# Trunk step: five kinds of tiles prefer the slots of the staying pool from the pools' exchange on

## The chip, the cores and the metric

The kernel runs on one core of a Trainium2 chip. Its engines work side by side, each through its own instructions in order: TensorE (PE, with its weight loads PEld), VectorE (DVE), ScalarE (ACT), GpSimd (POOL) and SyncE (SP), which here issues most of the DMA transfers. The metric is the device time of one execution in microseconds (us). Before the change it is 1383.22 us, the median of three runs (1382.85 to 1383.98).

## The reference

One layer of a hybrid decoder trunk for a prompt of 1024 rows and 8 sample rows (together NT = 1032 columns when x is held with the model dimension of 1024 on the partitions). Everything is float32.

```
h = rmsnorm(x, norm_pre) * (1 + scale) + shift
hA, cA, bA, zA, qkv, zB, beta, alpha, gA, gB = split(h @ w_in)
yA = ((bA * conv3(cA * hA)) * silu(zA)) @ w_out_a
q, k, v = split(silu(conv4(qkv)))            # 8 heads, q and k normalised
o, S = gated_delta_chunked(q, k, v, beta, g, s0)   # a recurrence over chunks
yB = (rmsnorm(o) * silu(zB)) @ w_out_b
merged = sigmoid(gA) * yA + sigmoid(gB) * yB
y = x + gate * rmsnorm(merged @ w_o, norm_post)
```

The recurrence is serial in each head: per chunk, the state S feeds a product, that feeds X and S again.

## The kernel before

**Stages.** After a start-up, the first long stage runs 48 *jobs*. A job multiplies h by 128 columns of w_in: 3 groups of 344 columns, each 24 matmuls into one of four pm_t banks (8 blocks of the model dimension, three products of high and low halves: xh·whi, xl·whi, xh·wlo). Its weights are loaded to wraw and split into whi and wlo (two buffers each). Eight heads take three jobs each (k, q, v) and their recurrences run as background work between the matmuls of later jobs. The other jobs are zB, and the 16 gate jobs for gB and gA (`gate_job`): their products are copied by ScalarE into a tile named gate, which is stored to memory (gBsc, gAsc) and read back much later. The last three jobs of all are gate jobs; their tiles are gate_9504, gate_9611 and gate_9724. The recurrence of the last head (its result is DA, its store yBsc<-DA) runs while the jobs before and the first of these three feed TensorE.

The second stage is `products`: the four parts of branch A for one group t of 128 columns are computed by a Strassen-like scheme of seven products, P1, P2, P6, P7, P4, P5, P3, on halves of rows and columns, 48 matmuls of 258 columns each, for eight groups. Their weights are loaded in four quarters to tiles wr, combined by VectorE and split to whi and wlo (`weight_load`, `weight_gen`). Their right sides are sums of blocks of x: `block_gen` builds tiles qa, qb and q1 from xh and xl, and splits them to thi and tlo. Result tiles are acc; they are combined and stored (yAsc). Meanwhile `park_gen` combines rows of yB from memory (pa_, pb_), splits them (phi, plo) and stores them (txs). Then `products_b` does the same seven products for w_out_b (rows read back to yraw, split to thi and tlo), and after it come the projection by w_out_a, the gates and w_o.

**Memory.** The tiles named so far take slots of `T4`, an object of class `Slots`. It has 7 slots t4 of 1056 columns in a pool that stays to the end, and 11 slots hb of the same width in the heads' pool bp, which also holds small tiles of the recurrence. At the start of the third last job, `to_products` drops the hb slots, releases bp, and puts a pool m into the same memory, with 22 slots sl of 1032 columns. A tile in m must wait until the last reader of whatever lay there in bp is done. `Slots.get` takes the free slot with the least key: the narrowest that is wide enough, and among equals an hb slot for the names in `LATE` and another for the rest.

**Order.** The program is written by strands that a clock model steps; `to_products` starts the strands weight_load, weight_gen and block_gen. A scheduler orders each engine's instructions afterwards, so where a tile lies decides also where its instructions stand.

Of the kernel before, what the change touches and what calls it, by code (L numbers as in the profile page):

```python
# [168 lines left out]
def hybrid_step(  # L169
# [442 lines left out]
    def start(gen):  # L612
        bg.append(Strand(gen, sched.cur.t if sched.cur else sched.clk["PE"]))
# [33 lines left out]
        return lambda: flags.get(key)  # L647

    LATE = ("gate", "lq")

    class Slots:

# [13 lines left out]
            return self.get(name, w)  # L666

        def get(self, name, w):
            i = min((i for i in self.free if i[2] >= w), key=lambda i: (i[2], ("hb" in i[1]) == (name in LATE)))
            self.free.remove(i)  # L670
            t = i[0].tile([P, i[2]], F32, tag=i[1], name=name)
            v = t[:, :w]
            self.held[id(v)] = (i, v)
            return v
# [71 lines left out]
    def drain_bg():  # L746
        force(lambda: not bg)
# [698 lines left out]
    def alloc(key, side):  # L1446
        pools[key] = tc.alloc_tile_pool(name=key, bufs=1, side=side)
        return pools[key]
# [3 lines left out]
    def weight_load(raw):  # L1452
        for key in list(range(SG, NK)) + ["B"]:
            w, n = (w_out_b, 2) if key == "B" else (w_in, 1)
            for odd, half in ((0, 0), (0, 1), (1, 0), (1, 1)):
                for g in range(n):
                    yield from when(lambda: len(raw) < 4 * n, lambda: T4.ready())
                    v = T4.get("wr", D)
                    for q in range(2):
                        c0 = (4 * g + 2 * q + odd) * P if n == 2 else ACOL[2 * q + odd] + key * P  # L1460
                        SY.dma_start(out=v[:, q * 512:(q + 1) * 512].rearrange("p (k c) -> p k c", c=P),
                                     in_=w[0, half * 512:(half + 1) * 512, c0:c0 + P]
                                     .rearrange("(k p) c -> p k c", p=P))
                    raw[key, odd, half, g] = v
                    yield

    def weight_gen(raw):

        sums = {}
        for n, (key, p, g) in enumerate(UNITS):  # L1470
            a11, a12, a21, a22 = ((key, o, hf, g) for o in range(2) for hf in range(2))
            src = {"P1": a11, "P2": a12, "P6": a11, "P7": a21, "P4": a22, "P5": None, "P3": a12}[p]
            yield from when(lambda: unit[0] >= n - 1, lambda: src is None or src in raw)
            hi_ = wpool.tile([P, NK, P], F32R, tag="whi", name="whi", bufs=2)
            lo_ = wpool.tile([P, NK, P], F32R, tag="wlo", name="wlo", bufs=2)
            hi, lo = (v.rearrange("p k c -> p (k c)") for v in (hi_, lo_))
            v = raw[src] if src else sums.pop(g)
            A.copy(out=hi, in_=v)
            yield
            tt(lo, v, hi.bitcast(F32), ALU.subtract)  # L1480
            made[key, p, g] = (hi_, lo_)
            yield
            if p == "P2":
                yield from when(lambda: a22 in raw and a21 in raw)
                s_ = wpool.tile([P, NK, P], F32, tag="wraw", name="wsum", bufs=2)
                s_ = sums[g] = s_.rearrange("p k c -> p (k c)")
                tt(s_, raw[a21], raw[a22], ALU.add)
                yield
                tt(raw[a21], raw[a11], raw[a21], ALU.subtract)
                tt(raw[a11], s_, raw[a11], ALU.subtract)  # L1490
                yield
                tt(raw[a12], raw[a12], raw[a11], ALU.subtract)
            elif p in ("P6", "P7", "P4", "P3"):
                T4.give(raw.pop(src))
# [239 lines left out]
    def to_products():  # L1734
        drain_bg()
        T4.free = [i for i in T4.free if i[0] is not bp]
        bp.release()
        T4.extend(alloc("m", "left"), "sl", NSL, NT)
        raw = {}
        for g in (weight_load(raw), weight_gen(raw), block_gen()):  # L1740
            start(g)
# [3 lines left out]

    isp = len(jobs)
    hook(isp - 3, to_products)
    hook(isp - 1, products_next)

# [128 lines left out]
    for j in range(9):  # L1878
        i, n, xr, mh, ml, held = pre.pop(j)
# [76 lines left out]
```

## Time and profile before

| what | us |
|---|---|
| median of three runs | 1383.22 |
| the profiled execution's own time | 1384.48 |
| its span in the profile | 1382.3 |
| last head's recurrence, in the span | about 722 to 743 |
| two last gate jobs and the rest of the third last | 753 to 775 |
| first product P1 begins | 775 |

The span is 1382.3 us, 2.2 less than the profiled execution's own time, and that execution is 1.26 above the median. The mean granted clock of TensorE is 0.994. Names in the profile have their numbers left out; all instructions go through one helper, so they bear the line L129 and are told apart by tiles. A row such as "A <- B" in a view of waits means that the instruction writing A waited for the one writing B.

### The profile page before, as it was taken

How to read it: one execution, taken by the hardware profiler on the slowest of the kernel's cores; microseconds unless marked ns; L12 is line 12 of the kernel's file. 1: busy time of each engine (PE TensorE's matmuls, PEld its weight loads, DVE VectorE, ACT ScalarE, POOL GpSimd, SP SyncE). 2: the span in 40 equal slices, each digit the busy share in tenths (PEclk: the TensorE clock that was granted, in tenths of full speed). 3: DMA queues.
4: the chain of work that ended last, by engine and by line, in shares of the span. 5: the costliest groups of instructions: out<-in, count | busy, mean ns of one | idle time of the engine just before them, and what ended most of it. 6: DMA issues, size and time to landing. Idle time of an engine off the chain costs nothing.

```text
span 1382.3 us, 26425 instructions
## 1 busy us (share of the span) xinstructions
PE 1347.6 (97%) x10257; PEld 1280.6 (93%) x10257; DVE 969.4 (70%) x2495; ACT 665.8 (48%) x1554; POOL 46.3 (3%) x98
## 2 busy tenths in 40 slices
PE   5999999999999999999998999999999999999997
PEld 2799999998999999999997999999999999899786
DVE  4667877676969476786645998777778867654553
ACT  5586685575757576564542534222333335332220
POOL 1000010000001000000000000000000200000000
PEclk9999999999999999999999999999999999999999
DMA  9533332332343233242442354422231866742221
GB/s 317 137 107 109 90 107 70 98 115 69 92 114 100 68 99 109 74 116 75 135 134 86 108 199 162 138 77 77 77 92 60 244 214 225 238 143 95 84 99 46
DMA packets 184928, 165.99 MB, mean 120 GB/s; under 512 B 33710, under 2 KB 158367, under 8 KB 184795
## 3 DMA queue, kind: packets, MB, share of 16 engines
q1 hardware_dynamic: 180216, 155.71, 36.7%
q0 software_dynamic: 4384, 8.52, 2.2%
q8 instruction: 81, 1.33, 0.4%
q14 instruction: 45, 0.36, 0.1%
q10 hardware_dynamic: 202, 0.08, 0.0%
HBM read 127.59 MB, written 36.91 MB: 119 GB/s over the span
## 4 chain that ended last, share of the span: by engine, by line
PE 79%; DVE 10%; DMA 5%; ACT 4%; issue 2%; SPq 1%; DVEq 0%; ACTq 0%
PE pm_t L129 54%; PE pa_t L129 22%; PE pb L129 3%; DVE wlo L129 2%; DVE kq L129 2%; DVE acc L129 1%; DVE Ts L129 1%; DVE Ttmp L129 1%; ACT junk L129 1%; DMA yAsc<-acc 1%; DMA xs<-in_x_prompt_dram 1%; SPq L129 1%; DMA Ts<-sT 1%; DVE vT L129 1%; DMA gcB<-gsc 1%
## 5 line engine op out<-in xcount | busy, mean ns | idle before, releaser
L129 PE MATMUL pm_t<-xh,whi 128*128 128x344 f32 (+1 forms) x1384 | 455.0, 329 | 4.8 <-ACT gate L129 4.4
L129 PE MATMUL pm_t<-xl,whi 128*128 128x344 f32 (+1 forms) x1384 | 435.7, 315 | 0.0
L129 PE MATMUL pm_t<-xh,wlo 128*128 128x344 f32 (+1 forms) x1384 | 435.6, 315 | 0.0
L129 PEld LDWEIGHTS pm_t<-xh,whi 128*128 128x128 f32 x1384 | 262.5, 190 | 8.2 <-ACT gate L129 4.6
L129 PEld LDWEIGHTS pm_t<-xl,whi 128*128 128x128 f32 x1384 | 262.6, 190 | 0.1
L129 PEld LDWEIGHTS pm_t<-xh,wlo 128*128 128x128 f32 x1384 | 261.9, 189 | 0.1
L129 ACT CAST whi<-wr 128x1024 fp32r<-128x1024 f32 x60 | 62.8, 1047 | 138.6 <-PE pm_t L129 67.3
L129 ACT CAST whi<-wraw 128x512 fp32r<-128x512 f32 x112 | 68.3, 626 | 57.3 <-PE pm_t L129 52.0
L129 DVE TENSOR_TENSOR wlo<-wraw,whi 128x512 fp32r<-128x512 f32 x112 | 75.8, 687 | 28.4 <-ACT whi L129 27.8
L129 PE MATMUL pm_t<-thi,wlo 128*128 128x258 f32 x304 | 85.8, 283 | 1.3 <-DVE wlo L129 1.3
L129 PE MATMUL pa_t<-thi,wlo 128*128 128x258 f32 x304 | 85.9, 283 | 0.6 <-DVE wlo L129 0.6
L129 PE MATMUL pa_t<-tlo,whi 128*128 128x258 f32 x304 | 86.0, 283 | 0.0
L129 PE MATMUL pm_t<-thi,whi 128*128 128x258 f32 x304 | 86.0, 283 | 0.0
L129 PE MATMUL pm_t<-tlo,whi 128*128 128x258 f32 x304 | 85.9, 283 | 0.0
L129 PE MATMUL pa_t<-thi,whi 128*128 128x258 f32 x304 | 85.9, 283 | 0.0
L129 DVE TENSOR_TENSOR wlo<-wr,whi 128x1024 fp32r<-128x1024 f32 x60 | 73.3, 1222 | 10.5 <-ACT whi L129 10.2
L129 PE MATMUL pa_t<-xh,whi 128*128 128x258 f32 x256 | 72.5, 283 | 0.0
L129 PE MATMUL pa_t<-xl,whi 128*128 128x258 f32 x256 | 72.5, 283 | 0.0
L129 PE MATMUL pa_t<-xh,wlo 128*128 128x258 f32 x256 | 72.3, 282 | 0.0
L129 DVE SCALAR_TENSOR_TENSOR kq<-raw,vecs,kq 128x528 f32<-128x528 f32 x96 | 70.4, 761 | 1.1 <-ACT kq L129 1.1
L129 ACT ACT_TABLE_LOAD x42 | 53.9, 1283 | 27.5 <-DVE kq L129 12.8
L129 PE MATMUL pm_t<-ylo,whi 128*128 128x344 f32 x192 | 61.7, 321 | 0.0
(377 smaller groups left out, 2956.2 us busy)
## 6 DMA issues: line engine op xcount, KB each, us to landing
wraw<-in_w_in_dram SPq DMA_DIRECT2D x48, 512.0 KB
wr<-in_w_in_dram SPq DMA_DIRECT2D x64, 256.0 KB
aw<-in_ada_w_dram SPq DMA_DIRECT2D x16, 512.0 KB
gBsc<-gate SPq DMA_DIRECT2D x8, 516.0 KB
gAsc<-gate SPq DMA_DIRECT2D x8, 516.0 KB
txs<-phi SPq DMA_DIRECT2D x8, 516.0 KB
txs<-plo SPq DMA_DIRECT2D x8, 516.0 KB
yAsc<-acc SPq DMA_DIRECT2D x8, 516.0 KB
```

Source lines behind the costliest of these rows:

```text
L129: r = f(*args, **kw)
```

## The change

From `to_products` on, five names (gate, wr, qa, qb, q1) take a free slot t4 ahead of any sl slot; before it, and for all other names, the order of slots is as it was. `EARLY` is empty until then.

```diff
     LATE = ("gate", "lq")
+    EARLY = []
...
         def get(self, name, w):
-            i = min((i for i in self.free if i[2] >= w), key=lambda i: (i[2], ("hb" in i[1]) == (name in LATE)))
+            i = min((i for i in self.free if i[2] >= w),
+                    key=lambda i: (not ("t4" in i[1] and name in EARLY), i[2], ("hb" in i[1]) == (name in LATE)))
             self.free.remove(i)
...
         T4.extend(alloc("m", "left"), "sl", NSL, NT)
+        EARLY.extend(("gate", "wr", "qa", "qb", "q1"))
         raw = {}
         for g in (weight_load(raw), weight_gen(raw), block_gen()):
             start(g)
```

Before, at that moment the narrower sl slots are preferred, so all of the named tiles lie in m. After, seven of the first ones lie in t4: wr_9475, qa_9478, qb_9479, q1_9480, gate_9504, qa_9556 and qb_9557, and then gate_9611 and qa_9701 in the slot that gate_9504 leaves. The tiles wr_9565, wr_9613, wr_9665, qa_9620, qb_9621, thi and tlo still lie in m.

ScalarE at the end of the last head. vn and DA are steps of its recurrence, whi_9627 the weights of the last gate job, whi_9694 those of P1. Before:

```order
L129 COPY vn_9427<-pa_t_9425 128x128
L129 COPY DA_7569<-pa_t_9421 128x128
L129 ACTIVATE junk_9435,so_9297<-pa_t_9421 128x128
L129 CAST whi_9627<-wraw_9469 128x512 x2
L129 COPY gate_9504<-pm_t_9471 128x344
L129 COPY gate_9504<-pm_t_9506 128x344
L129 COPY gate_9504<-pm_t_9546 128x344
L129 COPY gate_9611<-pm_t_9582 128x344
L129 CAST thi_9774<-qa_9478 128x516
```

The same place in the changed kernel, from the last steps of the head on:

```order
L129 COPY DA_7569<-pa_t_9421 128x128
L129 ACTIVATE junk_9435,so_9297<-pa_t_9421 128x128
L129 CAST whi_9627<-wraw_9469 128x512
L129 COPY gate_9504<-pm_t_9546 128x344
L129 CAST whi_9627<-wraw_9469 128x512
L129 COPY gate_9611<-pm_t_9582 128x344
L129 COPY gate_9611<-pm_t_9616 128x344
L129 CAST thi_9538<-qb_9479 128x516
L129 CAST thi_9538<-qb_9557 128x516
L129 CAST thi_9774<-qa_9478 128x516
L129 CAST thi_9774<-qa_9556 128x516
L129 CAST whi_9694<-wr_9475 128x1024
```

The first two copies to gate_9504 have moved up between the steps of the head (behind vn_9319 and ahead of vn_9391), the third and the first two of gate_9611 stand ahead of the first tile of the new pool, thi_9538.

VectorE in the change of head 6 to head 7, where S and X are steps of the recurrences and wlo the weights of a job, after the change:

```order
L129 TENSOR_TENSOR q1_9480<-qa_9478 128x516
L129 TENSOR_TENSOR qa_9478<-qb_9479,qa_9478 128x516
L129 TENSOR_TENSOR qb_9479<-qb_9479,q1_9480 128x516
L129 TENSOR_TENSOR wlo_9529<-wraw_9058,whi_9515 128x512
L129 TENSOR_TENSOR qb_9479<-qb_9479 128x516
L129 TENSOR_TENSOR wlo_9529<-wraw_9058,whi_9515 128x512
L129 TENSOR_TENSOR qa_9556<-xh_119,xl_120 128x1032
L129 COPY S_9306<-pa_t_9302 128x128
L129 TENSOR_TENSOR q1_9480<-qa_9556 128x516
L129 SCALAR_TENSOR_TENSOR X_9315<-pa_t_9311,nx_8192,vT_7734 128x128
```

Before, all of these sums stand behind the last write of DA, and behind the parking of a yB row:

```order
L129 SCALAR_TENSOR_TENSOR DA_7569<-pa_t_9458,vecs2_83,sz_8464 128x512
L129 TENSOR_TENSOR plo_10040<-pb__9809,phi_10039 128x1032
L129 TENSOR_TENSOR qa_9478<-xh_119,xl_120 128x1032
L129 TENSOR_TENSOR qb_9479<-xh_119,xl_120 128x1032
L129 TENSOR_TENSOR q1_9480<-qa_9478 128x516
L129 TENSOR_TENSOR qa_9556<-xh_119,xl_120 128x1032
L129 TENSOR_TENSOR qa_9478<-qb_9479,qa_9478 128x516
L129 TENSOR_TENSOR qb_9557<-xh_119,xl_120 128x1032
```

qa_9478 and qb_9479 themselves have moved further up, behind S_8929 and ahead of S_9111, two steps of head 6; the parking has moved down into the products.

SyncE's queue around the last head's store, before:

```order
L129 DMA gAsc_111<-gate_9124 128x1032
L129 DMA txs_114<-phi_10039 128x1032
L129 DMA out_4_dram<-S_9432 128x128
L129 DMA yBsc_113<-DA_7569 128x1024
L129 DMA txs_114<-plo_10040 128x1032
L129 DMA wr_9475<-in_w_in_dram 128x4x128 x2
L129 DMA wr_9565<-in_w_in_dram 128x4x128 x2
L129 DMA gAsc_111<-gate_9504 128x1032
```

And after:

```order
L129 DMA gAsc_111<-gate_9124 128x1032
L129 DMA out_4_dram<-S_9432 128x128
L129 DMA gAsc_111<-gate_9504 128x1032
L129 DMA yBsc_113<-DA_7569 128x1024
L129 DMA wr_9565<-in_w_in_dram 128x4x128 x2
L129 DMA wr_9613<-in_w_in_dram 128x4x128 x2
L129 DMA wr_9665<-in_w_in_dram 128x4x128 x2
L129 DMA gAsc_111<-gate_9611 128x1032
```

The store of gate_9504 now stands ahead of that of DA, and the load of wr_9475 has left the place for one some 17 transfers earlier.

## The prediction

> **What bounds the kernel now.** The page comes first: which engine is full, and whose work makes up the chain that ended last.
>
> ```profile
> PE 1347.6 (97%) x10257; PEld 1280.6 (93%) x10257; DVE 969.4 (70%) x2495; ACT 665.8 (48%) x1554; POOL 46.3 (3%) x98
> ...
> PE 79%; DVE 10%; DMA 5%; ACT 4%; issue 2%; SPq 1%; DVEq 0%; ACTq 0%
> ```
>
> TensorE is busy for 97% of the span, so a gain can only come from its waits and from time at a lower clock. The waits of TensorE, asked for in three stretches from 680 us on, show what there is to win (columns: total us, times, longest us).
>
> ```profile
> PE pm_t L129 <- ACT gate L129: 4.4, 1, 4.4
> PE pa_t L129 <- DVE wlo L129: 0.6, 1, 0.6
> PE pm_t L129 <- DVE wlo L129: 1.3, 1, 1.3
> ```
>
> The first lies in 680 to 800 us, the second in 800 to 1060, the third in 1060 to 1160. The first is by far the largest, and it is released by the very tile that the change moves. The chain of work that ended last says what the gate copy stood for.
>
> ```profile
> 748.48 1.42 DVE DA L129 x2
> ...
> 749.97 2.70 DMA yBsc<-DA
> ...
> 752.76 0.45 ACT gate L129
> ...
> 753.26 27.52 PE pm_t L129 x168
> 780.77 5.78 PE pa_t L129 x48
> ```
>
> The last head's output DA is written at 748.48, stored from 749.97 on, and only when that store has landed (2.70 us) ScalarE copies a bank of products into gate. The gate tile lies in memory that the heads' pool held; the store is the pool's last reader. The timeline shows what queues up there.
>
> ```profile
> 747.78 1.10 PE L129 MATMUL pa_t<-ident,DA 128*128 128x128 f32 x8 [0.20 <-DVE DA L129]
> ...
> 752.76 1.49 ACT L129 COPY gate<-pm_t 128x344 f32<-128x344 f32 x4 [7.94 <-DMA yBsc<-DA]
> ...
> 753.26 0.66 PE L129 MATMUL pm_t<-xh,whi 128*128 128x344 f32 x1 [4.38 <-ACT gate L129]
> ```
>
> Four copies run back to back: all four pm_t banks were full, and TensorE stood from 747.78 + 1.10 = 748.88 to 753.26, which is 4.38 us. Behind it the clock is low (windows: sum, PE, PEld, DVE, ACT, POOL busy, then granted clock, DMA share, GB/s; the second fence is of PE alone, with the clock after PE).
>
> ```profile
> 750.00:752.00 2.00, 0.00 (x0) 0.00 (x0) 1.16 (x1) 0.00 (x0) 0.00 (x0) 1.00 0.63 260
> 752.00:754.00 2.00, 0.74 (x2) 0.74 (x3) 1.22 (x2) 1.24 (x4) 0.00 (x0) 0.56 0.69 272
> ...
> 758.00:760.00 2.00, 2.00 (x11) 2.00 (x11) 2.00 (x4) 0.21 (x2) 0.00 (x0) 0.73 1.05 374
> ```
> ```profile
> 753.26:759.08 5.82, 5.82 (x20) 0.50 0.88 246
> ```
>
> A mean of 0.56 over 752 to 754 puts the fall at about 752.2, 3.4 us after TensorE's last matmul; a mean of 0.73 over 758 to 760 puts the rise at 758 + 1.08 = 759.1. So 5.8 us of matmuls ran at half clock.
>
> **The change, part by part.**
>
> *The gates leave the heads' memory.* gate_9504 and gate_9611 now take a slot of the pool that stays. Gate copies stand between the steps of the last head and before the first ScalarE operation that needs the released memory (a thi cast), so no bank is full when the transposes are done, and TensorE goes on into the second group of the last but one gate job. Removed: the 4.38 us of idle time, and with it the clock's fall. The 20 matmuls of the slow stretch took 5.82 us. At full clock they stand as these rows do:
>
> ```profile
> 764.01 0.32 PE L129 MATMUL pm_t<-xh,whi 128*128 128x344 f32 x1
> ...
> 765.89 0.32 PE L129 MATMUL pm_t<-xh,whi 128*128 128x344 f32 x1
> ```
>
> Those are 12 steps in 1.88 us, 0.157 us each; 20 x 0.157 = 3.1, so 2.7 us are lost. The chain's row gives it another way: its 168 matmuls are 120 of the gates (18.8 us at 0.157) and 48 of P1 (5.8, as the row below it), 24.6 against 27.52, so 2.9. I take 2.8. The first term is **−4.4 − 2.8 = −7.2 us**. A gap in TensorE that is left would cost its own length and, by the row of 752 to 754, nothing of the clock unless it passes some 3.4 us.
>
> The Trainium skill, TensorE: Matmul & The Clock Gate, section "What's actually happening", lets the clock rise after one busy window of about 3.4 us, from a window that runs freely; here the low stretch lasted 5.8 us. By the page's window the loss would be about half of 3.4, an estimate of 1.7, and the sum 1.1 smaller; the trace has the duration, so it decides.
>
> *The sums of x leave it too.* Here lies the second limit. Once the gates are free, VectorE has to have the sums, weights and their low halves for product P2 ready 7.2 us sooner. These rows are of VectorE's timeline before.
>
> ```profile
> 752.78 1.24 DVE L129 TENSOR_TENSOR qa<-xh,xl 128x1032 f32<-128x1032 f32 x1 [1.62 <-DMA yBsc<-DA]
> 753.93 1.23 DVE L129 TENSOR_TENSOR qb<-xh,xl 128x1032 f32<-128x1032 f32 x1
> 755.08 0.69 DVE L129 TENSOR_TENSOR q<-qa 128x516 f32<-128x516 f32 x1
> 755.68 1.23 DVE L129 TENSOR_TENSOR qa<-xh,xl 128x1032 f32<-128x1032 f32 x1
> ...
> 778.14 1.22 DVE L129 TENSOR_TENSOR wlo<-wr,whi 128x1024 fp32r<-128x1024 f32 x1
> ```
>
> A full-width operation takes 1.15 us from start to start, a half 0.60. VectorE began when the store had landed, and P2's low weights (778.14 + 1.22 = 779.4) were ready 1.4 us before P2 began at 780.77. After the change, three full operations and five halves stand earlier, before or inside the last head, 6.5 us in all, and one more full sum and three halves before the pool is free, in the 2.9 us that were idle or held the parking of another head's output. What is left between the release (about 752.8) and the end of P2's wlo is, in the changed order, 8 full operations and 15 halves: 9.2 + 9.0 = 18.2, so 771.0, or 771.5 with one wait for the first whi. P1 then starts at about 767.7 and P2 at 773.5. So 2 us are left, and this limit doesn't bind. Term: 0, and if each half-ready operand made VectorE wait, up to +2.
>
> *What they cost in the chain of heads 6 and 7.* The early operations go into engines that serve a serial recurrence, and each of their slots first waits for the store of the gate that held it. VectorE's and SyncE's rows:
>
> ```profile
> 692.66 0.35 DVE L129 SCALAR_TENSOR_TENSOR S<-S,egl,pa_t 128x128 f32<-128x128 f32 x1 [2.03 <-PE pa_t L129]
> ...
> 708.09 0.35 DVE L129 SCALAR_TENSOR_TENSOR S<-S,egl,pa_t 128x128 f32<-128x128 f32 x1 [2.19 <-PE pa_t L129]
> ...
> 723.62 0.29 DVE L129 COPY S<-pa_t 128x128 f32<-128x128 f32 x1 [2.27 <-PE pa_t L129]
> ```
> ```profile
> 689.42 0.34 SPq L129 DMA_DIRECT2D gAsc<-gate  x1
> ...
> 704.22 0.33 SPq L129 DMA_DIRECT2D gAsc<-gate  x1
> ```
>
> qa_9478 stands behind the S of 692.66 and waits for the store of 689.42; with the 2.70 us of the other store of this size it lands at 692.1, before S is done. qb_9479 stands ahead of the S of 708.09 and waits for the store of 704.22: 706.9 + 1.15 = 708.07, no slack but no loss. qa_9556 stands ahead of the copy at 723.62, which had 2.27 us of idle time before it: 1.15 fit. Bounds: 0 if all fit, 1.15 + 0.60 + 3 x 0.45 for three gate copies on ScalarE, 3.1 us, if nothing did. Since TensorE fills every step of these heads with gate matmuls, I take **+0.3**.
>
> *The weights' loads.* Of eight loads of first weights two are issued some 80 us earlier, six stay behind the release; SyncE gets no longer queue. In the products that follow, wr goes back to slots of the pool that stays, which only the five names prefer, instead of one that a result tile or a sum has just left. The chain before the second wait of TensorE, and before the third:
>
> ```profile
> 986.52 5.35 DMA yAsc<-acc
> ...
> 992.31 4.58 DMA wr<-in_w_in_dram
> ```
> ```profile
> 1109.78 6.39 DMA yAsc<-acc
> 1116.18 3.56 DMA yraw<-yBsc
> ```
>
> In the first, a weight load waited for a result tile's store, since it took that tile's slot. In the changed order it follows another wr in its slot and waits for that one's last reader, VectorE, alone: **−0.6**. In the second, a load of yB's rows waited for a result's store. The tiles yraw, yhi and ylo aren't named by the change and go on taking any slot; some loads come earlier, but a cast that waits for the store stands ahead of the weight cast. Bounds −1.3 (the wait goes) to +2.5 (most of a load of 3.56 goes into the path once more); I take **0**, the wait as it is.
>
> **Sum:** −7.2 + 0.3 − 0.6 = −7.5 us. Against the profiled execution (1384.48 us, of which 1382.3 are the span) that is 1377.0; this execution is 1.26 above the median, so beside the median of 1383.22 it is **1375.7**.
>
> **The rivals.**
>
> *A: part of the wait stays or comes back.* ScalarE works in order, and its thi casts wait for the release with the first product's whi and the third gate copy behind them; VectorE has its 18.2 us to do from the release on. If a landing later than 752.8, or waits between the two engines, made P2 late by 2 to 4 us beyond the 2 us of slack, the gain would be 3.5 to 5.5: 1377.7 to 1379.7. For it speaks that VectorE is full from 752.8 on; against it the 6.5 us that lie earlier.
>
> *B: slower, by stores in the recurrence.* At 2.70 us the stores cost nothing, but qb_9479 has no slack, and a store took 6.39 at 1109.78. At that price each of the waits of qa_9478, qb_9479 and the first gate copies puts up to 3.7 us into the path of the heads; three of them are 11, less 7.5: slower by 3.5, 1386.7. It decides from a landing of about 5.2 us on, where three waits eat the gain. Against it: a store of the same size took 2.70 in the stretch beside them, and what moves beside the early stores is one weight load of 512 KB; the 6.39 stand where the products' weights and sums are loaded.
>
> *C: it doesn't do what it says.* gate_9611 takes the same slot as gate_9504 and must wait for its store. Were that store issued behind the last head's, ScalarE would stand as before: 4 of the 4.38 us come back, the clock falls, and 1383 stays. Against it: SyncE's order has gate_9504's store ahead of yBsc's, and the copy that completes it stands between the two whi casts of this row, at about 744.4:
>
> ```profile
> 743.68 1.14 ACT L129 CAST whi<-wraw 128x512 fp32r<-128x512 f32 x2 [0.42 <-PE pm_t L129]
> ```
>
> With 0.45 for the copy and 2.70 for the store it lands by 747.7, and the free banks cover what is left.
>
> *D: more than forecast.* The third wait goes too and the chain costs nothing: 1374.1.
>
> **How the numbers follow.** Chances: forecast with its neighbourhood (gain 5.5 to 8.5) 0.60, D 0.08, A 0.18, C 0.08, B 0.06. A measurement of this kernel tells about 0.2%, 2.8 us, from no change. All of the forecast, D and nearly all of A lie below 1380.4; C and a little of A within; B above. That gives faster 0.85, same 0.09, slower 0.06. The range goes from 1373.4, which is D with 0.7 for the spread of runs, to 1380.5, A's far end with the same.
>
> **What would show it right or wrong.** In the changed profile, the wait of TensorE on ACT gate should be gone, the clock 1.00 in each window from 748 to 762, and P1's first product matmul at about 768. The S updates of heads 6 and 7 should follow each other as before; idle time of VectorE put down to gAsc would be B. TensorE waiting for DVE wlo or tlo at P2 or P6 (773 to 780) would be A. The wait near 1000 should be gone, that near 1122 there. The forecast is wrong if the gate tiles still wait for the release, or if the time comes back in a wait of TensorE later on.

## The result and the profile after

The changed kernel takes 1376.38 us, the median of six runs (1375.95 to 1376.98), beside 1383.55 for six runs of the kernel before (1382.85 to 1383.99): 7.2 us less, a ratio of 0.9948 with a 95% interval of 0.9935 to 0.9961. Its profiled execution took 1376.39 us, with a span of 1374.4. It lies on its median; that of before lies 0.9 above the median of six. The page's rows of engines and of the chain that ended last:

```profile
PE 1344.2 (98%) x10257; PEld 1277.8 (93%) x10257; DVE 970.0 (71%) x2495; ACT 664.8 (48%) x1554; POOL 46.3 (3%) x98
...
PE 83%; DVE 7%; ACT 4%; DMA 4%; issue 1%; SPq 0%; DVEq 0%; ACTq 0%
```

TensorE's share of the chain is up by 4 points, VectorE's down by 3. The waits of TensorE from 680 us on, in the stretches of before (680 to 800, then 1060 to 1160, then the rest; between 800 and 1060 there is none):

```profile
PE pa_t L129 <- DVE DA L129: 0.2, 1, 0.2
PE pm_t L129 <- DVE wlo L129: 2.1, 1, 2.1
PE pm_t L129 <- DVE ylo L129: 0.4, 1, 0.4
```

The wait of 4.4 us on the gate copy is gone, that of 0.6 too. A wait of 0.3 us on ACT vn at 679, just ahead of these stretches, is new; it comes up again under the prediction. The row of 1060 to 1160 reads like the one of before with a larger number, but it is another wait, as shown below. The chain of the changed kernel where the long wait was:

```profile
744.37 1.24 DVE DA L129
...
745.66 1.09 PE pa_t L129 x8
746.75 24.46 PE pm_t L129 x167
771.21 5.78 PE pa_t L129 x48
```

TensorE goes from the transposes straight into gate matmuls, and its 167 matmuls take 24.46 us, where 168 took 27.52. The windows say why: the clock is whole.

```profile
748.00:750.00 2.00, 2.00 (x15) 2.00 (x14) 1.93 (x3) 0.00 (x0) 0.00 (x0) 1.00 0.64 262
750.00:752.00 2.00, 2.00 (x15) 2.00 (x14) 1.97 (x3) 1.60 (x4) 0.00 (x0) 1.00 0.18 31
752.00:754.00 2.00, 2.00 (x15) 2.00 (x14) 2.00 (x4) 0.94 (x2) 0.00 (x0) 1.00 0.93 249
```

**A ledger.** Both programs have 10257 matmuls, of the same kinds in nearly the same order, so the n-th of one can be set beside the n-th of the other. The last column is the lead of the changed kernel; where it steps, time was won or lost.

```
   n   start before   start after   lead
   0         4.21          4.18     0.03
2265       313.93        314.02    -0.09
2330       319.68        317.71     1.97
5215       680.79        678.36     2.43
5217       681.06        679.18     1.88
5600       724.44        722.25     2.19
5751       748.61        746.37     2.24
5775       759.61        750.04     9.56
7745      1000.00        989.98    10.03
7760      1002.67        991.77    10.90
8560      1098.71       1087.74    10.97
8562      1098.96       1090.26     8.69
8590      1102.32       1095.22     7.11
8753      1122.04       1114.70     7.34
8760      1124.44       1115.53     8.91
9267      1186.13       1177.45     8.68
9300      1191.38       1183.31     8.07
last      1374.08       1366.09     7.98
```

These steps count. At 315 us, where no instruction is moved yet, the profiled execution of before has a lower clock, and that of after hasn't (one window of TensorE in each; the first row is of before):

```profile
314.00:318.00 4.00, 3.08 (x57) 0.67 0.00 0
314.00:318.00 4.00, 3.71 (x70) 1.00 0.00 0
```

These 2 us belong to the execution, not to the change, and so does a further 0.5 by 660 us. The first instructions that the change moves are two weight loads at 669 us; just behind them, at 681, 0.5 is lost, and 0.3 is won by 748. From 748 to 760 the lead grows by **7.3**, and by 1.4 more up to 1088, 0.9 of it at 1000. From there to 1095 **3.9** are lost, by 1124 1.8 are won, and 0.9 go after that. From 669 us on, where the lead is 2.43, the ledger makes 5.5 for the change; the medians make 7.2. The ledger compares two single executions, whose clock falls in different places; where in the other runs the 1.7 lie was not seen.

What is lost near 1090 reads so in the chain of the changed kernel; its VectorE and windows of TensorE alone follow.

```profile
1079.43 7.72 DMA wr<-in_w_out_b_dram
...
1089.07 1.15 DVE wlo L129
...
1090.26 1.82 PE pm_t L129 x9
```
```profile
1087.18 1.23 DVE L129 TENSOR_TENSOR wsum<-wr 128x1024 f32<-128x1024 f32 x1 [5.69 <-DMA wr<-in_w_out_b_dram]
1088.32 0.75 DVE L129 TENSOR_TENSOR acc<-pm_t,acc 128x258 f32<-128x258 f32 x2
1088.99 1.22 DVE L129 TENSOR_TENSOR wlo<-wr,whi 128x1024 fp32r<-128x1024 f32 x1
```
```profile
1088.00:1090.00 2.00, 0.14 (x2) 1.00 0.21 21
1090.00:1092.00 2.00, 1.74 (x10) 0.72 0.92 270
1092.00:1094.00 2.00, 2.00 (x11) 0.50 1.25 362
```

A weight load for `products_b` is issued at 1079 and takes 7.7 us; VectorE stands with a sum of weights at its head for 5.7 us, and the low half that the next product needs is queued behind. TensorE waits 2.1 us and then runs 3.4 us at half clock. The load was late in being issued, since SyncE stood waiting for VectorE's last read of the slot:

```profile
SPq L129 <- DVE wlo L129: 9.5, 1, 9.5
```

The half clock isn't in every run. A stretch of 3.4 us at half clock takes an estimated 0.0013 off the mean granted clock (1.7 of some 1345 us). The profiled execution has two, this one and one of 3.6 us behind its last matmul, and a mean of 0.997. Three of the other five runs have 0.999, which leaves room for one such stretch alone, and each of the eight profiles of this document has one of 3.5 to 5.5 us behind the last matmul. Yet these three runs took 1375.95 to 1376.48 us, at most 0.4 less than the profiled one; what they lose instead isn't seen. In the kernel before, the wait of this stretch came later, at 1122.

### The profile page after: what moved, and what is told of

Its sections match the earlier page's. It is cut to its first block, busy times and chain, and to the rows that moved or that the text cites. A ratio compares the mean times of both kernels' runs of the same rounds, so it can differ in the third digit from the quotient of the medians.

```text
span 1374.4 us, 26426 instructions
## 1 busy us (share of the span) xinstructions
PE 1344.2 (98%) x10257; PEld 1277.8 (93%) x10257; DVE 970.0 (71%) x2495; ACT 664.8 (48%) x1554; POOL 46.3 (3%) x98
## 3 DMA queue, kind: packets, MB, share of 16 engines
q8 instruction: 81, 1.33, 0.4%
## 4 chain that ended last, share of the span: by engine, by line
PE 83%; DVE 7%; ACT 4%; DMA 4%; issue 1%; SPq 0%; DVEq 0%; ACTq 0%
PE pm_t L129 57%; PE pa_t L129 23%; PE pb L129 3%; DVE kq L129 1%; DVE wlo L129 1%; ACT junk L129 1%; DMA xs<-in_x_prompt_dram 1%; DVE Ttmp L129 1%; DMA rB<-rsc 1%; DVE Ts L129 1%; DMA wr<-in_w_out_b_dram 1%; DMA gcB<-gsc 1%; SPq L129 0%; ACT DB L129 0%; ACT L129 0%
```

## The experiments

The theory had two parts. First, two limits lie close together at the pools' exchange: the gate tiles hold TensorE, and VectorE's sums hold P1 and P2; each part of the change moves one of them and neither is worth much alone. Second, the loss near 1090 comes from wr's part of the change. The first four runs leave out one part or leave one alone; each differs from the changed kernel in one line.

**Gates alone.**

```diff
-        EARLY.extend(("gate", "wr", "qa", "qb", "q1"))
+        EARLY.extend(("gate",))
```

> Only the gate tiles prefer the staying pool; weights and sums of x lie in the new pool as before the change. Theory (two limits: gates hold TensorE, then VectorE's sums hold P1 and P2): the 4.4 us wait on ACT gate and the low clock go, but VectorE starts its 6.5 us of early sums only at the release, so P1's low weights are ready near 769.8 and P2's near 779.4 on the scale of before, against a need at 767.7 and 773.5: TensorE waits about 6 us in all there, and the time is 1381 to 1384, within 3 us of before. Rival (the gates alone carry the gain, VectorE has room): no such wait, time 1375 to 1377.

Measured: 1381.34 us, median of 10 runs (1379.76 to 1383.06) beside 1383.29 (25 runs), ratio 0.9986 (0.9976 to 0.9996): 2 us of the 7. TensorE's waits at the first products, the windows of TensorE alone, and VectorE at the release and at P2's low weights:

```profile
PE pa_t L129 <- DVE wlo L129: 2.1, 1, 2.1
PE pm_t L129 <- ACT whi L129: 0.7, 1, 0.7
PE pa_t L129 <- ACT whi L129: 0.3, 1, 0.3
```
```profile
774.00:776.00 2.00, 0.82 (x6) 1.00 0.00 0
776.00:778.00 2.00, 2.00 (x14) 0.67 0.00 0
```
```profile
750.73 1.23 DVE L129 TENSOR_TENSOR qa<-xh,xl 128x1032 f32<-128x1032 f32 x1 [2.88 <-DMA yBsc<-DA]
...
773.90 1.22 DVE L129 TENSOR_TENSOR wlo<-wr,whi 128x1024 fp32r<-128x1024 f32 x1
```

The wait on the gate copy is gone and the lead over before grows from 2.2 to 9.5 us at 750, just as in the changed kernel. Then it falls to 3.8 by 787: VectorE starts its sums only when the store has landed, P2's low half is ready at 775.1, and the wait for it brings the low clock a second time. So the gates alone win 7.3 and lose 5.7 again. The total was as expected, the make-up not quite: P1 was late by 0.8 and not 2.1, and the clock took some 1.7 (half of 3.4) that the expectation hadn't in it.

**All but the gates.**

```diff
-        EARLY.extend(("gate", "wr", "qa", "qb", "q1"))
+        EARLY.extend(("wr", "qa", "qb", "q1"))
```

> wr, qa, qb and q1 prefer the staying pool, gate doesn't. Theory: the wait of TensorE on ACT gate (4.4 us) and the low clock behind it stay; the early sums gain nothing there; time 1382 to 1385 with the later waits as in the changed kernel (none near 1000, a new one of 2 us at the start of the products for w_out_b). Rival (the early sums and weights bring part of the gain): below 1380.

Measured: 1384.55 us (10 runs, 1382.88 to 1388.02), ratio 1.0011 (1.0002 to 1.0021). The two waits, at 750 and at 1100, are there:

```profile
PE pm_t L129 <- ACT gate L129: 4.7, 1, 4.7
PE pm_t L129 <- DVE wlo L129: 2.2, 1, 2.2
```

The early sums and weights alone win nothing, and carry the later loss. The clock didn't fall behind the wait of 2.2 us here:

```profile
1098.00:1100.00 2.00, 0.56 (x5) 1.00 0.00 0
1100.00:1102.00 2.00, 1.29 (x10) 1.00 0.94 202
```

**Gates and weights, without the sums.**

```diff
-        EARLY.extend(("gate", "wr", "qa", "qb", "q1"))
+        EARLY.extend(("gate", "wr"))
```

> gate and wr prefer the staying pool, the sums of x don't. Theory of two limits: as with the gates alone, VectorE is late by some 4 to 6 us at P2, so 1380 to 1383. Rival (gates alone, or gates with the first weights, carry it): 1375 to 1378.

Measured: 1383.47 us (10 runs), ratio 1.0000 (0.9990 to 1.0009), just above the expected range. The ledger has a lead of 8.4 us at 751 that falls to 3.5 by 787 and 2.3 by 829, the first part by the same waits as with the gates alone (2.1 us for wlo at P2 and a half clock), and the loss near 1100 comes on top. The rival, that gates and first weights carry the gain, is out by 5 us.

**Gates and sums, without the weights.**

```diff
-        EARLY.extend(("gate", "wr", "qa", "qb", "q1"))
+        EARLY.extend(("gate", "qa", "qb", "q1"))
```

> gate, qa, qb and q1 prefer the staying pool, wr doesn't. Theory: the first 7.2 us stay gained, since the first weights have time until 767; the wait near 1000 (0.6) comes back; the wait of 2.1 us at the first product for w_out_b near 1090, with its half clock of 3.4 us, goes, since it comes from the weights wr that now queue on their own slots; the wait of 1.3 near 1123 comes back. Time 1374 to 1376. Rival (the wait near 1090 has nothing to do with wr): it stays, time 1377 to 1379.

Measured: 1375.83 us (4 runs, 1374.36 to 1377.43), ratio 0.9947 (0.9932 to 0.9962): all of the gain. The lead grows by 7.6 between 748 and 760. The wait near 1090 is gone; those of TensorE from 1060 to 1160 are

```profile
PE pm_t L129 <- DVE wlo L129: 1.3, 1, 1.3
PE pm_t L129 <- ACT whi L129: 0.6, 1, 0.6
```

the first of them being that of before, at 1113 on this kernel's scale. The 0.6 near 1000 did not come back, against the expectation. It is in none of the six runs of this section, the gates alone included; so it isn't early weights that took it away, and what did stays open.

**Which weights.** Two runs part the early weights by stage; both start from the changed kernel. In the first, those of w_out_b alone go where they went before the change:

```diff
-                    v = T4.get("wr", D)
+                    v = T4.get("wb" if key == "B" else "wr", D)
```

> As the changed kernel, but the weights of w_out_b are loaded to tiles of another name, which doesn't prefer the staying pool; those of branch A keep it. Theory (the new wait of 2.1 us near 1090 comes from w_out_b's loads that wait for their own slots' last readers): it goes with its half clock, while the gain near 1000 (0.9) stays; the wait near 1120 of before may come back with 1.3. Time 1373 to 1375. Rival (the wait comes from the loads in a busy stretch of DMA wherever they lie): it stays, 1376 to 1377.

Measured: **1372.97 us** (5 runs, 1372.44 to 1373.89) beside 1383.29 (9 runs), ratio 0.9929 (0.9915 to 0.9942), just below the expected range. From 700 to 1130 TensorE has a single wait,

```profile
PE pa_t L129 <- DVE DA L129: 0.2, 1, 0.2
```

and neither the wait near 1090 nor that of 1120 is there. Matched with the changed kernel, matmul 8560 is 1.1 later (1.0 of it by 681 us, where the two kernels have the same instructions, so it belongs to the executions) and 8590 is 2.8 earlier: 3.9 won, as much as the ledger showed lost. SyncE's rows, first of the changed kernel, then of this one, show where the loads went:

```profile
1068.49 11.49 SPq L129 DMA_DIRECT2D wr<-in_w_out_b_dram  x4
```
```profile
1066.20 5.10 SPq L129 DMA_DIRECT2D yraw<-yBsc  x2
1071.76 5.94 SPq L129 DMA_DIRECT2D wb<-in_w_out_b_dram  x4
```

The last four transfers are all issued by 1077.7, and not by 1080. The runs together bear it out: the three kernels whose loads for w_out_b prefer slots of the staying pool (the changed one, all but the gates, gates and weights) lose 2.4 to 4.5 us here, and the other four that were changed lose nothing. This version beats both kernels. In the second run only the first group's weights are early:

```diff
-                    v = T4.get("wr", D)
+                    v = T4.get("wr" if key == SG else "ws", D)
```

> As the changed kernel, but only the weights of the first group prefer the staying pool; all later ones lie where they did before the change. Theory: as without early weights at all (1375.8): the gain at the gates stays, the later gains and losses of the weights go, 1375 to 1376.5. Rival (the first weights' early loads are what the gain rests on too): clearly below the kernel without early weights, under 1374.5.

Measured: 1378.28 us (5 runs, 1376.33 to 1378.50), ratio 0.9962 (0.9949 to 0.9974). Both theories missed. The profile has the wait of before near 1114, and this time the clock falls behind it:

```profile
PE pm_t L129 <- DVE wlo L129: 1.3, 1, 1.3
```
```profile
1114.00:1116.00 2.00, 0.91 (x6) 0.88 0.67 180
1116.00:1118.00 2.00, 2.00 (x11) 0.50 1.03 387
```

The kernel without early weights has the same wait at a whole clock. Step by step between these two profiled executions, the fall costs 1.5 us, and 0.9 are lost at 681, behind the early loads. But the profiled execution, at 1377.12 us, is 1.2 below its own median, so the 2.4 us between the two medians aren't explained by it. What is shown is that the first weights' early loads are not what the gain rests on.

The two runs also part the wait near 1120. It is gone where the later weights of branch A prefer the staying pool (the changed kernel, all but the gates, gates and weights, and the first run here), and it stays, at 1.1 to 1.3 us, where they don't (gates alone, gates and sums, and the second run here). So these weights earn the 1.8 us that the ledger has by 1124.

## Why the prediction was right

- *What bounds.* The wait on the gate copy, its release by the store and the half clock behind it were the large item, and they went: step by step 7.3 us against 7.2. This term, which is nearly the whole forecast, held to 0.1.
- *The second limit.* P2's low weights were worked out to be ready 2 us ahead of P2. In the changed kernel VectorE's row 

```profile
768.21 1.21 DVE L129 TENSOR_TENSOR wlo<-wr,whi 128x1024 fp32r<-128x1024 f32 x1
```

ends at 769.4, and P2 begins at 771.21: 1.8. That this limit is real, and that the early sums buy its slack, the two runs without them show: of the lead at 751, 5.7 us (gates alone) and 4.9 us (gates and weights) are gone by 787.
- *The chain of the heads.* +0.3 was forecast and 0.2 measured (2.43 to 2.24), but not by the way forecast, so this fit is luck. What costs time is the early weight loads, which the prediction put at nothing. They stand ahead of a small store (rsc, 4 KB) in SyncE's queue, and the load rB behind it reads what it stored. First the changed kernel, then before:

```profile
668.87 1.44 SPq L129 DMA_DIRECT2D wr<-in_w_in_dram  x2
671.01 0.30 SPq L129 DMA_DIRECT2D rsc<-sm_rT  x1
673.34 0.34 SPq L129 DMA_DIRECT2D rB<-rsc  x1
```
```profile
673.43 0.28 SPq L129 DMA_DIRECT2D rsc<-sm_rT  x1
674.76 0.32 SPq L129 DMA_DIRECT2D rB<-rsc  x1
```

rB is issued 2.33 us behind the store and not 1.33; ScalarE's work on rB and its vn come later with it, and TensorE waits for vn (the 0.3 at 679). In the five kernels with early first weights it is 2.3 to 2.6, and each loses 0.5 to 1.0 us at matmul 5217; in the three without (before, gates alone, gates and sums) it is 1.3, and neither of the latter two loses anything there. The early sums and gates cost nothing that shows. (Of free slots of one width, the names in `LATE` take one that is not an hb slot, and the rest an hb slot first; so the gates lay in t4, and the sums wait for their stores.) The sum without slack did wait for such a store, and its successor was 0.1 late (706.10 with the lead of 2.1 there, against 708.09):

```profile
704.95 1.23 DVE L129 TENSOR_TENSOR qb<-xh,xl 128x1032 f32<-128x1032 f32 x1 [1.18 <-DMA gAsc<-gate]
706.10 0.34 DVE L129 SCALAR_TENSOR_TENSOR S<-S,egl,pa_t 128x128 f32<-128x128 f32 x1
```

The store was issued at 702.16, so it landed in 2.8 us: rival B's price of 6.39 did not come up there.
- *The weights near 1000.* −0.6 was predicted, −0.9 measured at that place (10.03 to 10.90) and −1.4 over the whole stretch. The reason isn't the one given, weights that follow weights in a slot: the wait is gone in all six experiments, those without early weights too. What took it away stays open.
- *The start of `products_b`.* Here the step failed. It was put at 0, the wait near 1120 as it was. That wait went (−1.8), and the loads of w_out_b, which wait for slots of the staying pool, brought another of 2.1 us with a half clock, +3.9; together +2.1, inside the bound of +2.5 but by another mechanism than the one named, a load of weights and not of yB's rows. Both causes are shown: with the loads of w_out_b put back the new wait is gone, and the one near 1120 stays wherever the later weights of branch A aren't early. Of the 3.9, the 1.6 of the half clock isn't in every run.
- *After 1124* the kernel loses 0.9, of which 0.4 is the new wait on ylo; it was not foreseen and not followed up.
- *The clock.* That a gap under some 3.4 us leaves it alone was wrong (below).

The terms measured are +0.2 − 7.3 − 1.4 + 3.9 − 1.8 + 0.9 = −5.5 in the two profiled executions, against −7.5 forecast and −7.2 between the medians. The first term was right in size and in mechanism. The terms behind it were forecast at −0.3 and measured at +1.8 together, so that the medians come within 0.3 of the forecast is in part luck.

## What to carry to other kernels

When a new pool takes the place of an old one, look for the tile whose first writer stands at the head of an engine's queue: it makes the engine wait for the old pool's last store, and a tile in memory that stays doesn't wait for that store. Then ask for the second limit behind it: here the gates alone won 2 us, sums and weights without the gates nothing, and gates and sums together 7. A preference for slots should end where its reason ends: the same rule, left on for the loads of w_out_b, cost some 3 us of what could be had (7.2 won, against 10.3 without it). And a load that is issued early should be looked at in the queue where it then stands: two of them held up a small store that a serial chain needs.

## What the runs showed of the hardware

A wait of TensorE costs its own length, or some 1.7 us more for each stretch of low clock behind it, and its length alone doesn't say which. The clock fell for 3.4 us behind waits of 2.1 us (the changed kernel at 1090, the gates alone at 776) and of 1.3 us (at 1115, first weights alone), and didn't behind one of 2.2 us (at 1100, without the gates) or of 1.3 us (before, at 1122). The falls of one execution lie on a grid: in the profile of before the clock is low from 315.34 to 318.76 and from 752.25 to 759.08, and 752.25 − 315.34 is 128 times 3.413. So it seems to count how the gap lies to that grid. These are stretches of it with TensorE alone: ahead of the fall at 1090 (changed kernel), ahead of the time near 1124 where none came, and the first of the two low ones from 752 (both before).

```profile
1087.46:1090.88 3.42, 1.30 (x11) 1.00 0.26 39
1120.89:1124.30 3.41, 2.13 (x17) 1.00 0.33 69
752.25:755.66 3.41, 2.40 (x8) 0.50 0.82 262
```

The stretch ahead of a fall had TensorE busy for 1% (before, 749), 38% (the changed kernel, 1087.5), 44% (gates alone, 773), 21% and 39% (gates and weights), but also 57% and 65% in two cases; stretches of 53% (without the gates, 1097) and of some 62% (twice) were followed by none, and none above 65% was. So the share doesn't part them cleanly either. The clock rose again each time behind a stretch that was busy throughout; behind the two low ones in which TensorE was busy for 70% (before) and 61% (without the gates) it stayed low. The Trainium skill, TensorE: Matmul & The Clock Gate, section "What's actually happening", has the same free-running window of 3413 ns; that it takes an idle window to bring the fall is not borne out here, since six falls came behind windows that were 21 to 65% busy.
